# Turning the input of a two-layer decoder trunk once, and giving VectorE the low parts of the weights in three stages

## The chip, the cores and the metric

The kernel runs on one core of a Trainium2 chip, as one launch. The metric is the device time of one execution in microseconds (us), taken over several runs; a profile is one more execution of the same program, with its own time.

## The reference, cut to what matters

Two layers on x of 1024 tokens by 1024 features, all in fp32. Layer 0 is an mLSTM mixer and a squared-ReLU MLP, layer 1 is latent attention on shared keys and values and the same kind of MLP. The change touches layer 0's mixer and its first residual:

```python
cond = silu(c)
sh1, sc1, g1, sh2, sc2, g2 = split(cond @ ada_w[0] + ada_b[0], 6)      # adaLN vectors
h = rmsnorm(x, norm_g[0, 0]) * (1 + sc1) + sh1                         # first normalisation
q, k, v, ig, fg, og = split(h @ w_in)                                  # 8 heads
hh = mlstm_chunkwise(q, k, v, ig + b0, fg + b1)                        # chunks of 128 tokens
y = (rmsnorm(hh, head_g) * sigmoid(og)) @ w_out
x = x + g1 * rmsnorm(y, norm_g[0, 1])                                  # first residual
h2 = rmsnorm(x, norm_g[0, 2]) * (1 + sc2) + sh2
x = x + g2 * rmsnorm(sqrelu_mlp(h2), norm_g[0, 3])
# layer 1: the same frame around latent attention, then its MLP
```

## The kernel before

Tokens go in two halves of 512. Activations lie with features on the partitions: a tensor of one half is 8 blocks (`KD`) of 128 features by 512 tokens. The input arrives with tokens on the partitions and so has to be turned, 128 by 128, by TensorE.

**Split precision.** Each fp32 operand of a product is kept as a high part (a ScalarE cast to the reduced fp32 kind of TensorE, `hi`) and a low part (x - hi, `lo`). A product (`mm3`, L236 to L238) is three matmuls: low weight by high activation, high by low, high by high. An activation's low part is made by VectorE or GpSimd. A weight comes in blocks of 512 KB on SyncE's DMA queue (`wload`, issue at L216) into one of four buffers `raw`; `wsplit` then lets ScalarE cast the high part (`wh`, L193) and VectorE or GpSimd, taking turns, make the low part (`wl`, L195). A list of one entry, `low[0]`, names one engine for all low parts while it is set. There is room for four split weights.

**Layer 0 up to the first residual**, in the order of the program:

1. `vector_columns` and the load of half 0's x (`x0`, L299). `first_norm`: ScalarE squares the rows (L496), VectorE scales each row by its rstd (L503), TensorE turns the scaled rows (32 transposes, L524), ScalarE copies them into `xT0` (L1655).
2. `ada_first(j)` makes the first adaLN vectors for features 512j to 512j + 511, from weight columns loaded beside (TensorE products L326 and L338, VectorE sums L363/L365). `modulate0(…, j)` then makes u = xT * A + sh on VectorE (L1662), the high part on ScalarE (L1663), the low part (L1665). Half 0's q/k products (`qk_pairs`) run in two halves of the features around this.
3. `gates_in` (the gates' product), woven with steps of `bgs`, the background stream that makes the other adaLN vectors out of 512 KB blocks (loads L358 into the same `raw` buffers, VectorE multiply-adds L365 into `tma`, transposes L345, sum L347).
4. `load_x1` (half 1's x), then `v_in` (products for v) woven with `intra0` (chunk-local part of the mLSTM: gate chains on 8 partitions around L701 to L786, small products L749 to L772) and `bgs`.
5. `scale_x1` (squares L510, scaling L520 on VectorE and GpSimd), then `in_turn` lays side by side the output gates `og0` of half 0, the chunk recurrence `chunks0` and, as a fill advanced at two of three steps, `norm0`: half 1's transposes (L530) into PSUM, one ScalarE activation that scales and shifts (L532), and the two parts (L534 to L538).
6. Half 1: `gates_in`, then q/k and v products woven with `intra0`, `split_o` (o split in parts, L784 to L786) of half 0 and `bgs`.
7. `wout` of half 0 beside `chunks0` of half 1; then `og0` of half 1 with `split_o` of half 1 and `p0`; then `wout` of half 1 woven with `p0`. `p0 = post(...)` is half 0's residual (`residual`, add at L941) and second normalisation (`normed`, L478 to L485). Half 1's, `p1`, runs inside the MLP of half 0.

The residual takes its x from a source: `x_rows` loads the rows once more (L895) and turns each block with four transposes (L901) into PSUM; layer 1 and the MLPs use `x_ahead`, which loads 512 KB blocks of the running x^T from a DRAM scratch `xs`.

**What sets the order.** A scheduler lays the instructions of each engine in one fixed order by its own estimate of times; priorities (`prompt`), `issue_after` and `paced` push it. Each engine and SyncE's DMA queue work through their lists in that order; a DMA that waits for a buffer holds all that stand behind it. PSUM has tags `ps`, `pc` and `pm` with two buffers each (`pm` has two banks). SBUF tags are `tmp` (3), `tmc` (6), `k4` (24), `hd` (8).

Of the kernel before, what the change touches and what calls it, by code (L numbers as in the profile page):

```python
# [17 lines left out]
P = 128  # L18
# [29 lines left out]
def drain(*gens):  # L48
    for g in gens:
        for _ in g:  # L50
            pass
# [31 lines left out]
def kernel(  # L83
# [42 lines left out]
    def hd(dt=F32):  # L126
        return sb.tile([P, 1024], dt, tag="hd", bufs=HD, name=f"hd_{next(uid)}")
# [10 lines left out]
    def tmc(dt=F32):  # L138
        return sb.tile([P, 512], dt, tag="tmc", bufs=TMC, name=f"tmc_{next(uid)}")
# [4 lines left out]
    def small(n, dt=F32):  # L144
        return sb.tile([P, n], dt, tag=f"sm{n}", bufs=6, name=f"sm_{next(uid)}")
# [4 lines left out]
    def pc():  # L150
        return pp.tile([P, 512], F32, tag="pc", bufs=2, name=f"pc_{next(uid)}")

    def pm():
        return pp.tile([P, 2, 512], F32, tag="pm", bufs=2, name=f"pm_{next(uid)}")

    def const(shape, dt, name):
        return sb.tile(shape, dt, tag=name, bufs=1, name=name)
# [271 lines left out]
    def rsqrt_(y, v, t):  # L429

        nc.scalar.activation(t, v, AF.Ln)
        nc.scalar.activation(y, t, AF.Exp, scale=-0.5)
        nc.vector.tensor_mul(t, y, y)
        nc.vector.scalar_tensor_tensor(t, t, -0.5, v, ALU.mult, ALU.mult)
        nc.vector.scalar_tensor_tensor(y, t, 1.5, y, ALU.add, ALU.mult)
# [53 lines left out]
            if k % 4 == 3:  # L489
                yield 1  # L490

    def scale_rows(xt):
        st = small(4)
        for t in range(4):
            junk = pm()
            nc.scalar.activation(  # L496
                junk.rearrange("p a b -> p (a b)"), xt[t], AF.Square, accum_out=st[:, t : t + 1]
            )
        v, y, w = small(4), small(4), small(4)
        nc.vector.tensor_scalar(v, st, 1.0 / D, EPS, ALU.mult, ALU.add)  # L500
        rsqrt_(y, v, w)
        for t in range(4):
            nc.vector.tensor_scalar(xt[t], xt[t], y[:, t : t + 1], None, ALU.mult)  # L503

    def scale_x1(x1):
# [7 lines left out]
        v, y, w = small(4), small(4), small(4)  # L513
        nc.vector.tensor_add(v, st[:, 0:4], st[:, 4:8])
        nc.vector.tensor_scalar(v, v, 1.0 / D, EPS, ALU.mult, ALU.add)
        rsqrt_(y, v, w)
        for g in range(2):
            for t in range(4):
                e = nc.gpsimd if t % 2 else nc.vector
                e.tensor_scalar(x1[g][t], x1[g][t], y[:, t : t + 1], None, ALU.mult)  # L520

    def turn(xt, pt, k):
        for t in range(4):
            nc.tensor.transpose(pt[:, ts(t, P)], xt[t][:, ts(k, P)], ident)  # L524

    def norm0(h, xt, A, sh):
        for k in range(KD):
            pt = ps()
            for t in range(4):
                nc.tensor.transpose(pt[:, ts(t, P)], xt[k // 4][t][:, ts(k % 4, P)], ident)  # L530
            u = tmc()
            nc.scalar.activation(u, pt, AF.Identity, bias=sh[:, k : k + 1], scale=A[:, k : k + 1])  # L532
            if k % 2:
                nc.vector.tensor_copy(h.hi[k], u)  # L534
            else:
                nc.scalar.copy(h.hi[k], u)
            e = nc.vector if k % 2 else nc.gpsimd
            e.tensor_sub(h.lo[k], u, h.hi[k].bitcast(F32))  # L538
            yield


# [121 lines left out]
    def og0(hf, alloc):  # L663
        hf.gs = FH(F32, alloc)
        for k in range(NH):
            pt = proj_fm(w_in, 2064 + k * P, hf.h)
            g = hf.gs[k]
            nc.scalar.activation(g, pt, AF.Exp, scale=-1.0)
            nc.scalar.activation(g, g, AF.Ln, bias=1.0)
            nc.scalar.activation(g, g, AF.Exp, scale=-1.0)  # L670
            nc.vector.tensor_scalar(g, g, col(HG + k, 1), None, ALU.mult)
            yield
# [206 lines left out]
    def wout(w, o, store, wide=False):  # L879

        for m in range(KD):
            pt = proj_fm(w, m * P, o, (lambda: pm()[:, 0]) if wide and m % 2 else ps)
            store(m, pt)
            yield


    xs = scratch([D, S], "xs")
    xs_blk = lambda k, half: xs[ts(k, P), ts(half, H)]

    def x_rows(half):  # L890

        xt = []
        for t in range(4):
            a = hd() if half else k4()[:, :1024]
            nc.sync.dma_start(a, x_of[half * 4 + t])  # L895
            xt.append(a)

        def blk(k):
            pt = pc()
            for t in range(4):  # L900
                nc.tensor.transpose(pt[:, ts(t, P)], xt[t][:, ts(k, P)], ident)  # L901
            return pt

        return blk

    def x_cols(half):
        def blk(k):
# [3 lines left out]

        return blk

    def x_ahead(alloc):


        def src(half):
            t = [alloc() for _ in range(4)]
            for b in range(4):
                nc.sync.dma_start(  # L920
                    t[b], xs[2 * b * P : (2 * b + 2) * P, ts(half, H)].rearrange("(k p) n -> p k n", p=P)
                )
            return lambda k: t[k // 2][:, k % 2]

        return src
# [721 lines left out]

    def first_norm():

        scale_rows(x0)  # L1650
        xT = FH(claim=True)
        for k in range(KD):
            pt = pc()
            turn(x0, pt, k)
            nc.scalar.copy(xT[k], pt)  # L1655
        return xT

    def modulate0(h, xT, j):
        A, sh = A0, adac(0, SH1)
        for k in range(4 * j, 4 * j + 4):  # L1660
            u = tmc()
            nc.vector.tensor_scalar(u, xT[k], A[:, k : k + 1], sh[:, k : k + 1], ALU.mult, ALU.add)  # L1662
            nc.scalar.copy(h.hi[k], u)  # L1663
            e = nc.gpsimd if j and k % 2 else nc.vector
            e.tensor_sub(h.lo[k], u, h.hi[k].bitcast(F32))  # L1665
            yield

    def w_raw(b):
# [7 lines left out]
        return [t.rearrange("p (a b) -> p a b", b=256) for t in wsplit(r, D)]  # L1676

    vector_columns()
    xT0 = first_norm()
    drain(ada_first(0, k4))  # L1680

    w0 = [w_raw(b) for b in range(3)]
# [26 lines left out]
    def in_turn(wide, steps, fill):  # L1709

        traced = nc.cur_bb.bb.instructions
        last = [None]

        def go(gen):
            top = traced[-1]
            if last[0] is None:
                r = next(gen, StopIteration)
            else:
                with tc.issue_after(last[0]):
                    r = next(gen, StopIteration)  # L1720
            for i in reversed(traced):
                if i is top:
                    break
                if i.engine == pe_last[0].ins.engine:
                    last[0] = i
                    break
            return r

        n = 0
        while go(steps) is not StopIteration:  # L1730

            if n % 3 < 2:
                go(wide)
                next(fill, None)
            n += 1
        drain(wide)

    bgs = chain(bg0, bg1)
    drain(qk_pairs(hfs[0], w0, modulate0(hfs[0].h, xT0, 1)))
    drain(with_bg(gates_in(hfs[0]), bgs, 1))  # L1740
    x1 = load_x1()
    drain(weave(with_bg(v_in(hfs[0]), bgs, 1), intra0(hfs[0]), 1.5))
    scale_x1(x1)
    hfs[1].h = Split()
    n1 = norm0(hfs[1].h, x1, A0, adac(0, SH1))
# [235 lines left out]
```

## Time and profile before

| | us |
|---|---|
| three runs | 2413.01, 2415.41, 2417.33 |
| their median | 2415.41 |
| the profiled execution | 2414.08 |
| its span in the trace | 2412.3 |

In the profile PE is TensorE's matmuls, PEld its weight loads, DVE is VectorE, ACT ScalarE, POOL GpSimd, SP SyncE, and SPq a DMA queue's own waits. L12 is line 12 of the kernel. A group row reads: line, engine, operation, out<-in, partitions by elements, count, then busy time, mean ns, and the idle time of the engine ahead of these with what ended it. A timeline row has the start, the busy time, and the instruction; brackets give the idle time ahead of it. PEclk is the granted TensorE clock as a share of full speed.

### The profile page before, as it was taken

The page shows a single profiled execution, that of the slowest core. Times are in us where ns is not written, and L with a number is a line of the kernel's source. Part 1 is how long each engine was busy: PE and PEld are TensorE (multiplying, and loading weights), DVE is VectorE, ACT ScalarE, POOL GpSimd, SP SyncE. Part 2 cuts the span into 40 slices and gives each one's busy share as a digit, 9 for nine tenths or more (in the row PEclk, how much of TensorE's full clock was granted, in tenths as well). Part 3 has the DMA queues.
Part 4 walks back from the last instruction along what each step waited for, and adds up shares of the span by engine and source line. Part 5 has one row for each costly group of instructions (what it writes and reads, how often), then busy time and mean ns, then how long its engine had stood idle before and what let it go on. Part 6 is the DMA issues. An engine that isn't in the chain of part 4 may idle for free.

```text
span 2412.3 us, 30656 instructions
## 1 busy us (share of the span) xinstructions
PE 2369.8 (98%) x11669; PEld 1950.5 (81%) x11669; DVE 1476.4 (61%) x2269; ACT 1049.5 (44%) x1706; POOL 435.5 (18%) x269
## 2 busy tenths in 40 slices
PE   7999999999999999999999999999999999999998
PEld 5887787788888887888888877888888888888886
DVE  6576766958665667866664967554555385253335
ACT  4355334645333354434444554434444443443333
POOL 2131221300000000233421100332221102121121
PEclk9999999999999999999999999999999999999999
DMA  7442564444654745555543454774424454354431
GB/s 267 147 130 63 176 191 131 150 133 141 197 175 130 246 133 182 155 168 176 185 131 110 145 161 153 243 250 139 157 97 135 119 162 122 109 188 134 143 103 62
DMA packets 373843, 370.30 MB, mean 154 GB/s; under 512 B 24163, under 2 KB 282272, under 8 KB 373696
## 3 DMA queue, kind: packets, MB, share of 16 engines
q1 hardware_dynamic: 373408, 368.24, 48.6%
q8 instruction: 92, 1.51, 0.3%
q14 instruction: 55, 0.45, 0.1%
q0 software_dynamic: 288, 0.10, 0.0%
HBM read 313.24 MB, written 55.05 MB: 153 GB/s over the span
## 4 chain that ended last, share of the span: by engine, by line
PE 88%; DVE 6%; DMA 3%; ACT 2%; issue 1%; POOL 0%; SPq 0%; DVEq 0%; ACTq 0%
PE ps L236 16%; PE ps L237 16%; PE ps L238 16%; PE pm L236 9%; PE pm L238 9%; PE pm L237 9%; DMA raw<-in_mlp_w_dram 2%; PE pc L1456 1%; PE pc L236 1%; PE pm L811 1%; PE pc L238 1%; PE pc L237 1%; PE pm L1342 1%; PE pm L1336 1%; PE pm L1338 1%
## 5 line engine op out<-in xcount | busy, mean ns | idle before, releaser
L193 ACT CAST wh<-raw 128x1024 fp32r<-128x1024 f32 (+2 forms) x366 | 375.8, 1032 | 740.2 <-PE ps L236 356.3
L195 POOL TENSOR_TENSOR wl<-raw,wh 128x1024 fp32r<-128x1024 f32 (+2 forms) x158 | 379.8, 2409 | 1522.3 <-ACT wh L193 1356.7
L236 PE MATMUL ps<-k,wl 128*128 128x512 f32 x1528 | 611.4, 400 | 6.5 <-DVE wl L195 3.3
L237 PE MATMUL ps<-k,wh 128*128 128x512 f32 x1528 | 601.5, 394 | 0.0
L238 PE MATMUL ps<-k,wh 128*128 128x512 f32 x1528 | 600.8, 393 | 0.0
L195 DVE TENSOR_TENSOR wl<-raw,wh 128x1024 fp32r<-128x1024 f32 (+1 forms) x208 | 270.0, 1301 | 285.1 <-ACT wh L193 278.1
L236 PEld LDWEIGHTS ps<-k,wl 128*128 128x128 f32 x1528 | 287.0, 188 | 74.3 <-DVE wl L195 5.0
L238 PEld LDWEIGHTS ps<-k,wh 128*128 128x128 f32 x1528 | 287.0, 188 | 67.5 <-issue 0.5
L237 PEld LDWEIGHTS ps<-k,wh 128*128 128x128 f32 x1528 | 287.4, 188 | 63.0 <-issue 1.9
L203 DVE TENSOR_TENSOR k<-k,pm 128x512 f32<-128x512 f32 (+1 forms) x254 | 210.7, 859 | 130.3 <-PE pm L238 129.5
L476 DVE TENSOR_TENSOR hd<-tmp,hd 128x512 fp32r<-128x512 f32 x128 | 120.9, 945 | 205.5 <-ACT hd L475 205.2
L236 PE MATMUL pm<-hd,wl 128*128 128x512 f32 x512 | 201.8, 394 | 0.5 <-ACT hd L475 0.5
L237 PE MATMUL pm<-hd,wh 128*128 128x512 f32 x512 | 199.7, 390 | 0.7 <-DVE hd L476 0.7
L238 PE MATMUL pm<-hd,wh 128*128 128x512 f32 x512 | 200.0, 391 | 0.0
L236 PE MATMUL pm<-wh,hd 128*128 128x512 f32 x488 | 192.4, 394 | 2.8 <-ACT raw L1348 2.5
L237 PE MATMUL pm<-wl,hd 128*128 128x512 f32 x488 | 191.3, 392 | 0.0
L238 PE MATMUL pm<-wh,hd 128*128 128x512 f32 x488 | 191.1, 392 | 0.0
L365 DVE SCALAR_TENSOR_TENSOR tma<-raw,cond,tma 128x512 f32<-128x512 f32 x168 | 130.4, 776 | 20.9 <-DMA raw<-in_ada_w_dram 12.1
L1348 ACT ACTIVATE raw<-pm,sm 128x128 f32<-128x128 f32 (+3 forms) x64 | 47.4, 741 | 157.0 <-DVE sm L1347 126.7
L237 PEld LDWEIGHTS pm<-hd,wh 128*128 128x128 f32 x512 | 96.2, 188 | 21.6 <-DVE hd L476 1.0
L236 PEld LDWEIGHTS pm<-hd,wl 128*128 128x128 f32 x512 | 96.1, 188 | 21.4 <-ACT hd L475 0.9
L238 PEld LDWEIGHTS pm<-hd,wh 128*128 128x128 f32 x512 | 96.1, 188 | 21.0
(359 smaller groups left out, 3603.2 us busy)
## 6 DMA issues: line engine op xcount, KB each, us to landing
raw<-in_mlp_w_dram SPq DMA_DIRECT2D x256, 512.0 KB, 4.3
raw<-in_ada_w_dram SPq DMA_DIRECT2D x80, 512.0 KB, 4.4
raw<-in_a_w_in_dram SPq DMA_DIRECT2D x48, 512.0 KB, 4.6
xs<-k SPq DMA_DIRECT2D x40, 256.0 KB, 4.6
raw<-in_kv_ada_w_dram SPq DMA_DIRECT2D x16, 512.0 KB, 4.0
raw<-in_a_w_out_dram SPq DMA_DIRECT2D x16, 512.0 KB, 4.7
kd<-k SPq DMA_DIRECT2D x32, 256.0 KB, 3.5
vd<-k SPq DMA_DIRECT2D x32, 256.0 KB, 5.0
```

What stands on the lines that cost most here:

```text
L193: nc.scalar.copy(hi[:, :n], r[:, :n])
L195: i = e.tensor_sub(lo[:, :n], r[:, :n], hi[:, :n].bitcast(F32))
L203: return f(*a, **k)
L236: nc.tensor.matmul(o, ll, rh, start=start, stop=False)
L237: nc.tensor.matmul(o, lh, rl, start=False, stop=False)
L238: pe_last[0] = nc.tensor.matmul(o, lh, rh, start=False, stop=stop)
L365: nc.vector.scalar_tensor_tensor(acc, r[:, kk], cond[:, k : k + 1], acc, ALU.mult, ALU.add)
L476: nc.vector.tensor_sub(lo, u, hi.bitcast(F32))
L811: nc.tensor.matmul(nv[:, r, i], hf.PT[p_][:, r, cs], v[:, 2 * p_ + r], start=g == 0, stop=True,)
L1336: nc.tensor.matmul(o[:, :w], ql, kh, start=True, stop=False)
L1338: nc.tensor.matmul(o[:, :w], qT, kk[1][:, ks], start=False, stop=False)
L1348: nc.scalar.activation(pr[:, :n], f, AF.Exp, bias=m, scale=SCALE, accum_out=l)
```

## The change

- The rows of x are no longer scaled. `rms_x0` and `rms_x1` give only rstd per token; `along_tokens` spreads it over the partitions (four matmuls with the identity and a ScalarE copy), and the modulation multiplies by it: u = xT * A * rstd on VectorE in one instruction, then `split_mod` makes the high part with the shift on ScalarE and the low part on VectorE, for every block.
- x^T is kept in two DRAM scratches `xt_d`: half 0's four blocks of 512 KB behind the first q/k products in the program, half 1's eight blocks of 256 KB out of `norm0`, which now copies each turned block out of PSUM first.
- The first residual of both halves reads x^T from there by `x_ahead(…, True)`; `x_rows` is gone.
- `low[0]` is VectorE in `v_in`/`intra0` of half 0 and from `gates_in` to `v_in`/`intra0` of half 1.
- `gates_in` of half 0 is no longer woven with `bgs`.
- `in_turn` advances its fill at each step.
- Half 1's output gates alternate between `ps` and one bank of `pm` (`one_pm`).

```diff
+    def one_pm():
+        return pm()[:, 0]
...
-    def scale_rows(xt):
+    def along_tokens(dst, y):
+        pt = pc()
+        for t in range(4):
+            nc.tensor.matmul(
+                pt[:, ts(t, P)], y[:, t : t + 1].to_broadcast([P, P]), ident, start=True, stop=True
+            )
+        nc.scalar.copy(dst, pt)
+        return dst
+    def rms_rows(v):
+        nc.vector.tensor_scalar(v, v, 1.0 / D, EPS, ALU.mult, ALU.add)
+        y, w = small(4), small(4)
+        rsqrt_(y, v, w)
+        return y
...
-        v, y, w = small(4), small(4), small(4)
-        nc.vector.tensor_scalar(v, st, 1.0 / D, EPS, ALU.mult, ALU.add)
-        rsqrt_(y, v, w)
-        for t in range(4):
-            nc.vector.tensor_scalar(xt[t], xt[t], y[:, t : t + 1], None, ALU.mult)
+        return rms_rows(st)
...
-        for g in range(2):
-            for t in range(4):
-                e = nc.gpsimd if t % 2 else nc.vector
-                e.tensor_scalar(x1[g][t], x1[g][t], y[:, t : t + 1], None, ALU.mult)
...
-    def norm0(h, xt, A, sh):
+    xt_d = [scratch([D, H], f"xt{i}") for i in range(2)]
+    def norm0(h, xt, y, A, sh):
+        rstd = along_tokens(tmp(), y)
         for k in range(KD):
             pt = ps()
-            for t in range(4):
-                nc.tensor.transpose(pt[:, ts(t, P)], xt[k // 4][t][:, ts(k % 4, P)], ident)
-            u = tmc()
-            nc.scalar.activation(u, pt, AF.Identity, bias=sh[:, k : k + 1], scale=A[:, k : k + 1])
-            if k % 2:
-                nc.vector.tensor_copy(h.hi[k], u)
-            else:
-                nc.scalar.copy(h.hi[k], u)
-            e = nc.vector if k % 2 else nc.gpsimd
-            e.tensor_sub(h.lo[k], u, h.hi[k].bitcast(F32))
+            turn(xt[k // 4], pt, k % 4)
+            a, u = tmp(), tmc()
+            nc.scalar.copy(a, pt)
+            nc.sync.dma_start(xt_d[1][ts(k, P)], a)
+            nc.vector.scalar_tensor_tensor(u, pt, A[:, k : k + 1], rstd, ALU.mult, ALU.mult)
+            split_mod(h.hi[k], h.lo[k], u, sh[:, k : k + 1])
             yield
...
-            pt = proj_fm(w_in, 2064 + k * P, hf.h)
+            pt = proj_fm(w_in, 2064 + k * P, hf.h, one_pm if hf.i and k % 2 else ps)
...
-    def x_rows(half):
...
-    def x_ahead(alloc):
+    def x_ahead(alloc, first=False):
         def src(half):
             t = [alloc() for _ in range(4)]
+            of = xt_d[half] if first else xs[:, ts(half, H)]
             for b in range(4):
                 nc.sync.dma_start(
-                    t[b], xs[2 * b * P : (2 * b + 2) * P, ts(half, H)].rearrange("(k p) n -> p k n", p=P)
+                    t[b], of[2 * b * P : (2 * b + 2) * P].rearrange("(k p) n -> p k n", p=P)
                 )
...
-        scale_rows(x0)
+        y = rms_x0(x0)
...
-        return xT
+        return xT, along_tokens(Cst.rearrange("p a b -> p (a b)")[:, :H], y)
...
             u = tmc()
-            nc.vector.tensor_scalar(u, xT[k], A[:, k : k + 1], sh[:, k : k + 1], ALU.mult, ALU.add)
-            nc.scalar.copy(h.hi[k], u)
-            e = nc.gpsimd if j and k % 2 else nc.vector
-            e.tensor_sub(h.lo[k], u, h.hi[k].bitcast(F32))
+            nc.vector.scalar_tensor_tensor(u, xT[k], A[:, k : k + 1], rs0, ALU.mult, ALU.mult)
+            split_mod(h.hi[k], h.lo[k], u, sh[:, k : k + 1])
...
             if n % 3 < 2:
                 go(wide)
-                next(fill, None)
+            next(fill, None)
...
     drain(qk_pairs(hfs[0], w0, modulate0(hfs[0].h, xT0, 1)))
-    drain(with_bg(gates_in(hfs[0]), bgs, 1))
+    for b in range(4):
+        nc.sync.dma_start(
+            xt_d[0][2 * b * P : (2 * b + 2) * P].rearrange("(k p) n -> p k n", p=P), xT0.t[b]
+        )
+    drain(gates_in(hfs[0]))
     x1 = load_x1()
+    low[0] = nc.vector
     drain(weave(with_bg(v_in(hfs[0]), bgs, 1), intra0(hfs[0]), 1.5))
-    scale_x1(x1)
+    low[0] = None
+    y1 = rms_x1(x1)
...
+    low[0] = nc.vector
     drain(gates_in(hfs[1]))
...
     drain(weave_n(with_bg(main, bgs, 1.7), intra0(hfs[1]), 0.8))
+    low[0] = None
...
-    p0 = post(hfs[0], y0, B0, x_rows, A1, adac(0, SH2))
+    p0 = post(hfs[0], y0, B0, x_ahead(k4v, True), A1, adac(0, SH2))
...
-    p1 = post(hfs[1], y1, B0, x_rows, A1, adac(0, SH2))
+    p1 = post(hfs[1], y1, B0, x_ahead(hdv, True), A1, adac(0, SH2))
```

More of the change, by code (lines that the diff above doesn't have):

```diff
@@ L490, in normed, with rms_x0 @@
                 yield 1
-    def scale_rows(xt):
+    def along_tokens(dst, y):
[11 more added lines that the diff above has]
+        return y
+    def rms_x0(xt):
         st = small(4)
@@ L498, in scale_rows, with rms_x1 @@
             )
-        v, y, w = small(4), small(4), small(4)
-        nc.vector.tensor_scalar(v, st, 1.0 / D, EPS, ALU.mult, ALU.add)
-        rsqrt_(y, v, w)
-        for t in range(4):
-            nc.vector.tensor_scalar(xt[t], xt[t], y[:, t : t + 1], None, ALU.mult)
-    def scale_x1(x1):
+        return rms_rows(st)
+    def rms_x1(x1):
         st = small(8)
@@ L512, in scale_x1 @@
                 )
-        v, y, w = small(4), small(4), small(4)
+        v = small(4)
         nc.vector.tensor_add(v, st[:, 0:4], st[:, 4:8])
-        nc.vector.tensor_scalar(v, v, 1.0 / D, EPS, ALU.mult, ALU.add)
-        rsqrt_(y, v, w)
-        for g in range(2):
-            for t in range(4):
-                e = nc.gpsimd if t % 2 else nc.vector
-                e.tensor_scalar(x1[g][t], x1[g][t], y[:, t : t + 1], None, ALU.mult)
+        return rms_rows(v)
     def turn(xt, pt, k):
@@ L881, in wout @@
         for m in range(KD):
-            pt = proj_fm(w, m * P, o, (lambda: pm()[:, 0]) if wide and m % 2 else ps)
+            pt = proj_fm(w, m * P, o, one_pm if wide and m % 2 else ps)
             store(m, pt)
@@ L888 @@
     xs_blk = lambda k, half: xs[ts(k, P), ts(half, H)]
-    def x_rows(half):
[L892 to L904, printed above, removed]
     def x_cols(half):
@@ L1678 @@
     vector_columns()
-    xT0 = first_norm()
+    xT0, rs0 = first_norm()
     drain(ada_first(0, k4))
@@ L1739 @@
     drain(qk_pairs(hfs[0], w0, modulate0(hfs[0].h, xT0, 1)))
-    drain(with_bg(gates_in(hfs[0]), bgs, 1))
+    for b in range(4):
[3 more added lines that the diff above has]
+    drain(gates_in(hfs[0]))
     x1 = load_x1()
+    low[0] = nc.vector
     drain(weave(with_bg(v_in(hfs[0]), bgs, 1), intra0(hfs[0]), 1.5))
-    scale_x1(x1)
+    low[0] = None
+    y1 = rms_x1(x1)
     hfs[1].h = Split()
-    n1 = norm0(hfs[1].h, x1, A0, adac(0, SH1))
+    n1 = norm0(hfs[1].h, x1, y1, A0, adac(0, SH1))
     in_turn(og0(hfs[0], hdv), chunks0(hfs[0]), n1)
     drain(n1)
+    low[0] = nc.vector
     drain(gates_in(hfs[1]))
```

## The prediction

> **What bounds the kernel now.** I read the page's busy shares and its chain first, then busy time by window, then TensorE's waits, then the timelines of the places where TensorE waits.
>
> ```profile
> span 2412.3 us, 30656 instructions
> PE 2369.8 (98%) x11669; PEld 1950.5 (81%) x11669; DVE 1476.4 (61%) x2269; ACT 1049.5 (44%) x1706; POOL 435.5 (18%) x269
> PE 88%; DVE 6%; DMA 3%; ACT 2%; issue 1%; POOL 0%; SPq 0%; DVEq 0%; ACTq 0%
> ```
>
> TensorE is busy 98% of the span and is 88% of the chain. So a gain is either TensorE work taken out, or one of TensorE's few waits. The windows (us, then busy us of PE, PEld, DVE, ACT, POOL, granted clock, DMA share, GB/s) and the waits (total, times, longest) show where these are.
>
> ```profile
> 0.00:25.00 25.00, 11.86 (x58) 7.45 (x58) 14.23 (x39) 13.24 (x23) 6.36 (x21) 1.00 0.95 337
> 117.70:121.10 3.40, 1.52 (x9) 0.99 (x9) 3.40 (x6) 2.81 (x8) 2.67 (x1) 1.00 0.61 186
> 121.10:124.50 3.40, 3.40 (x18) 3.40 (x17) 1.55 (x2) 0.31 (x1) 0.00 (x0) 0.50 0.88 273
> 124.50:127.90 3.40, 3.40 (x31) 2.92 (x30) 1.75 (x4) 2.82 (x6) 2.38 (x1) 1.00 0.56 194
> 150.00:225.00 75.00, 75.00 (x452) 61.10 (x452) 49.70 (x126) 39.87 (x86) 22.73 (x13) 1.00 0.23 64
> 250.00:275.00 25.00, 22.60 (x126) 16.88 (x126) 18.63 (x36) 8.07 (x17) 2.58 (x5) 1.00 0.55 160
> 300.00:375.00 75.00, 75.00 (x543) 66.13 (x542) 49.39 (x101) 25.09 (x53) 14.91 (x6) 1.00 0.60 178
> 425.00:450.00 25.00, 25.00 (x127) 20.65 (x126) 23.73 (x31) 16.58 (x25) 7.00 (x3) 1.00 0.60 184
> 450.00:475.00 25.00, 25.00 (x110) 20.07 (x109) 24.47 (x33) 17.22 (x26) 9.22 (x11) 1.00 0.36 111
> 500.00:525.00 25.00, 25.00 (x112) 20.04 (x111) 16.62 (x23) 12.78 (x20) 0.00 (x0) 1.00 0.24 71
> ```
>
> ```profile
> PE pc L524 <- DVE k L503: 5.2, 1, 5.2
> PE ps L236 <- DVE wl L195: 3.3, 3, 1.6
> PE ps L236 <- ACT k L203: 1.6, 1, 1.6
> PE ps L237 <- POOL wl L195: 1.3, 1, 1.3
> PE pc L749 <- ACT tmc L756: 0.5, 1, 0.5
> PE pc L338 <- DVE tmc L365: 0.4, 1, 0.4
> PE pc L338 <- DVE ada L341: 0.3, 1, 0.3
> ```
>
> Wherever the change reaches, TensorE waits only at the start, around 70, around 118 and between 250 and 275. From 150 to 225 and from 300 to 375 it never stops.
>
> **Transposes of the residual's x: -7.0.** The 64 transposes of L901 go; x^T comes by DMA instead, in as many loads of 512 KB as the x rows took.
>
> ```profile
> L901 PE MATMUL pc<-ident,k x32: 270/272/273, 427.0 to 447.1; 128*128 128x128 f32 x32
> L901 PE MATMUL pc<-ident,hd x32: 270/272/273, 517.0 to 542.3; 128*128 128x128 f32 x32
> ```
>
> ```profile
> 440.32 0.39 PE L236 MATMUL ps<-k,wl 128*128 128x512 f32 x1
> 441.01 0.60 PE L901 MATMUL pc<-ident,k 128*128 128x128 f32 x4
> 441.36 0.48 PE L236 MATMUL ps<-k,wl 128*128 128x512 f32 x1
> 442.14 0.39 PE L236 MATMUL ps<-k,wl 128*128 128x512 f32 x1
> ```
>
> A duration of 0.272 overlaps its neighbours, so I price by starts. Four transposes move the next matmul by 441.36 - 441.01 = 0.35, and the triple behind them takes 0.78 instead of 0.69: 0.44 for a block. Two halves of 8 blocks: 16 x 0.44 = 7.0. The second half (517 to 542) leaves in full, since VectorE is at 16.62 of 25 there. In the first, VectorE is busy 23.73 + 24.47 = 48.20 of 50: TensorE may shed 1.8 of its 3.5 before VectorE is the bound, so up to 1.7 comes back; there the output product of half 1 also waits for VectorE's and GpSimd's split of its operand. I take +0.5 (0 to +1.7): TensorE shows no wait there, which speaks for the low end.
>
> **The start: -0.7 (+1 to -5.2).** x is no longer scaled before it is turned, so the 5.2 wait for L503 goes. But the DMA engines hold the pace (tenths of busy share, slices of 1.5 us, then GB/s):
>
> ```profile
> DMA  0599999999999999999999999999390000065038
> GB/s 0 98 391 354 398 371 375 385 391 391 386 386 384 351 348 356 379 389 388 385 385 392 393 312 348 354 345 167 37 302 23 0 0 0 0 156 194 0 60 281
> ```
>
> ```profile
> 27.89 0.50 PE L236 MATMUL pm<-k,wl 128*128 128x512 f32 x1 [1.49 <-ACT k L1663]
> 39.05 1.02 PE L338 MATMUL pc<-ones,tmc 128*128 128x1 f32 x8 [0.37 <-DVE tmc L365]
> 26.64 1.92 DVE L1662 TENSOR_SCALAR tmc<-k,mods,ada 128x512 f32<-128x512 f32 x4
> L485 DVE SCALAR_TENSOR_TENSOR hd<-hd,mods,tmc 128x512 f32<-128x512 f32 x8 | 5.4, 748 | 0.0
> ```
>
> Loads run without a gap to 42, and the first modulation, for which the first q/k matmul waits at 27.89, needs the adaLN vectors that they bring. The transposes only move into time in which TensorE waits for data anyway. What is left are two waits behind VectorE (0.4 + 0.3), which has the scaling less to do: -0.7. Against it, the modulation's first step becomes a scalar_tensor_tensor: 0.748 instead of 1.92 / 4 = 0.48, four times +0.27, hence the +1. Spreading rstd along the tokens is eight matmuls more (0.44 for four): the first four lie in that wait, the other four stand in half 1's normalisation: **+0.4**.
>
> The store of x^T (2 MB, at 386 GB/s 5.4 us) stands on SP's queue ahead of the weights of the second half of the q/k products. The DMA engines fall quiet at 45 and stay so to 52, so the stores fit, and those weights land as late as 49. An estimate from this row gives about 1 us of slack: 0, at worst +3.
>
> **The stalls around 70 and 118: -1.65, -1.9, -1.4.** In both a weight of v_in comes late.
>
> ```profile
> 67.64 1.05 ACT L193 CAST wh<-raw 128x1024 fp32r<-128x1024 f32 x1 [8.42 <-DMA raw<-in_a_w_in_dram]
> SPq L216 <- DVE tma L365: 31.4, 4, 26.3
> 117.45 2.91 POOL L195 TENSOR_TENSOR wl<-raw,wh 128x1024 fp32r<-128x1024 f32 x1 [34.83 <-ACT wh L193]
> ```
>
> At 67.64 ScalarE's queue stood 8.42 at a cast whose weight was loaded behind adaLN blocks; the evictions behind it held TensorE's PSUM for 1.6 (waits, L203). Now gates_in of half 0 draws no adaLN steps, and in the changed kernel's instruction order the weight loads stand ahead of them: the 1.65 goes. At 117, SP's queue (waits from 50 to 125) had waited 26.3 for the raw buffer that VectorE's L365 frees, then GpSimd took 2.91 for the low part. In the new order the pair behind that wait is loaded and split ahead of the chain of the gates, with the low part on VectorE: 0.5 + 1.3 of waits, or 3.40 - 1.52 = 1.9, goes.
>
> Right behind this stall the granted clock was 0.50 for 3.4 us: 18 matmuls instead of 31. At full speed they take 18 x 3.40 / 31 = 1.97, so 1.43 was lost. I take it that the slow stretch follows the stall (-1.4); if not, 0. [...]
>
> **VectorE makes the low parts in both v_in/intra stages: +0.5 (-3.3 to +3).**
>
> ```profile
> L195 POOL TENSOR_TENSOR wl<-raw,wh 128x1024 fp32r<-128x1024 f32 (+2 forms) x158 | 379.8, 2409 | 1522.3 <-ACT wh L193 1356.7
> L195 DVE TENSOR_TENSOR wl<-raw,wh 128x1024 fp32r<-128x1024 f32 (+1 forms) x208 | 270.0, 1301 | 285.1 <-ACT wh L193 278.1
> L195 DVE TENSOR_TENSOR wl<-raw,wh 128x1024 fp32r<-128x1024 f32 x10 | 15.6, 1561 | 16.4 <-ACT wh L193 16.4
> L195 POOL TENSOR_TENSOR wl<-raw,wh 128x1024 fp32r<-128x1024 f32 x9 | 22.3, 2478 | 96.5 <-ACT wh L193 96.5
> ```
>
> The last two rows are 250 to 375 alone. Nine low parts move to VectorE, 9 x 1.30 = 11.7; its ten there fall from 1.56 to 1.30, since GpSimd's no longer run beside them, and give back 2.6. VectorE has room: 18.63 of 25 and 49.39 of 75. A weight's low part comes in 1.3 instead of 2.4, but behind whatever VectorE has queued, the gates' chain included. Best, the three waits on VectorE's low parts go (-3.3); worst, two of 1.5 stand in a row (+3); +0.5 since TensorE has no wait from 300 on.
>
> [...]
>
> **Half 1's normalisation: +0.3 (0 to +3).** A PSUM bank is now released by a ScalarE copy and a VectorE multiply (0.75) instead of one activation; VectorE has 49.70 of 75 and TensorE no wait there, so I take half a block. x^T's eight stores stand on SP between w_in loads; at 0.23 DMA share nothing waits. Output gates alternating between PSUM kinds: 0, hidden by the same full TensorE.
>
> **Sum:** -7.0 + 0.5 - 0.7 + 0.4 - 1.65 - 1.9 - 1.4 + 0.5 + 0.3 = -10.95. The profiled execution took 2414.08; that gives 2403.1. The three runs shown have their median 1.3 above it (2415.41): **2404.5**. A measurement of this kernel can tell about 0.2%, 4.8 us.
>
> **Rivals.**
> *Slower: VectorE becomes the bound in half 1's q/k and v_in.* The 10 + 9 weights of 250 to 375 each come one low part late, SP's weight loads queueing behind raw buffers that VectorE frees: 19 x 1.30 = 24.7, 2429. It decides once VectorE reaches 25 of 25 in these windows; for it, three waits on its L195 already; against, 68 of 100 busy plus 9.1. Chance 0.11.
> *Little change: the stalls form again elsewhere* (the adaLN blocks still hold the raw buffers, and must come sometime) and VectorE takes 1.7 in 425 to 475: 1.65 + 1.9 + 1.4 + 1.2 = +6.2, 2410.7. For it, the 26.3 wait is no shorter by itself; against, the weights' new places ahead. Chance 0.21.
> *The x^T store delays the q/k weights,* +3, and a half-clock stretch of 1.4 behind it: 2408.9. Chance 0.08.
> *The start's wait goes in full,* 4.5 more: 2400. Against it, the DMA row. Chance 0.10.
> *The transposes cost nothing now* (they fill gaps): 2411.5; excluded by 25.00 of 25 busy and the shift of 0.44.
>
> **How the numbers follow.** Forecast 0.50 (2401 to 2408 with its bounds), the rest as above. Faster by over 0.2% (under 2410.6): forecast, start, store and nearly half of the second rival, 0.77; slower (over 2420.2): 0.09; same 0.14. The range takes in all but the slower rival and the tail of little change: low 2397 (the start's case with 3 of low-part waits gone), high 2414.
>
> **What would show it.** Right: no L901 in the trace and PE's count lower by about 56; no PE wait at 68 to 70 nor 117 to 121; clock 1.00 from 100 to 125; PE still full from 425 to 475; the first q/k matmul near 27.5. Wrong: VectorE at 24 or more of 25 in 250 to 375 with TensorE waiting for wl; a TensorE wait near 50 behind a DMA; waits for split_o's blocks near 455.

## The result, and the profile after

| | before | after |
|---|---|---|
| median, us (22 runs each) | 2415.59 | 2418.04 |
| lowest to highest | 2413.01 to 2418.51 | 2416.45 to 2422.01 |
| span of the profile | 2412.3 | 2415.3 |

The ratio is 1.0012 (95% interval 1.0006 to 1.0017): slower by 0.12%, a small loss that is clear of the spread of these runs. A gain of 11 us was forecast, to 2404.5, and the range ended at 2414.

The page of the changed kernel, its span, busy shares and chain:

```profile
span 2415.3 us, 30563 instructions
PE 2368.1 (98%) x11621; PEld 1946.3 (81%) x11621; DVE 1488.3 (62%) x2283; ACT 1050.3 (43%) x1712; POOL 396.7 (16%) x247
PE 83%; DVE 7%; DMA 6%; ACT 3%; issue 1%; POOL 0%; SPq 0%; DVEq 0%; ACTq 0%
```

TensorE's share of the chain fell from 88 to 83%. Less work is in the kernel, and more waiting. Two windows of before, and then windows of after (us, then busy us of PE, PEld, DVE, ACT, POOL, granted clock, DMA share, GB/s):

```profile
50.00:125.00 75.00, 71.48 (x441) 61.41 (x440) 40.53 (x70) 23.75 (x47) 10.61 (x9) 0.98 0.46 149
225.00:300.00 75.00, 71.24 (x414) 58.68 (x413) 59.07 (x95) 26.42 (x51) 16.75 (x10) 1.00 0.50 152
```

```profile
50.00:125.00 75.00, 75.00 (x496) 66.08 (x495) 46.78 (x75) 26.08 (x55) 3.50 (x6) 1.00 0.46 149
225.00:300.00 75.00, 73.98 (x462) 61.41 (x461) 61.50 (x99) 27.17 (x55) 8.31 (x6) 1.00 0.50 155
425.00:450.00 25.00, 22.57 (x97) 17.67 (x95) 24.48 (x28) 12.89 (x19) 13.85 (x3) 1.00 0.73 223
450.00:475.00 25.00, 19.71 (x74) 14.79 (x74) 22.52 (x29) 17.43 (x28) 8.16 (x10) 0.93 0.20 64
475.00:500.00 25.00, 22.33 (x88) 18.13 (x89) 12.41 (x10) 8.43 (x12) 5.40 (x2) 0.86 0.49 128
700.00:725.00 25.00, 23.04 (x96) 18.43 (x96) 18.61 (x24) 9.69 (x12) 0.00 (x0) 0.93 0.60 180
```

The stalls around 70 and 118 are gone, as forecast: TensorE is full from 50 to 125. Those between 225 and 300 have become smaller. But from 425 to 500, where it never stopped before but for 0.7, it idles, and for part of that time it runs at half clock (0.50 from 454.67 to 458.08 and from 475.16 to 481.99). A fresh stall stands at 717. TensorE's waits of the changed kernel from 420 to 500 (total, times, longest):

```profile
PE ps L239 <- POOL wl L198: 5.4, 1, 5.4
PE ps L239 <- ACT k L796: 2.2, 1, 2.2
PE pc L469 <- DVE tmc L465: 1.8, 1, 1.8
PE ps L240 <- POOL k L797: 1.0, 1, 1.0
```

To add up by stage I use TensorE's time over its floor: the time from each matmul's start to the next's, less the usual distance for its width in these traces (0.228 us for 512 columns, 0.172 for 384, 0.117 for 256, 0.108 for 130, 0.109 for 128, else 0.05), summed over one profile. It holds waits and half clock alike, and leaves the matmuls themselves out. The last two columns are two experiments told below.

| us of the span | before | after | bg_three | bg3_low |
|---|---|---|---|---|
| 0 to 50 | 19.6 | 18.3 | 19.4 | 18.3 |
| 50 to 125 | 7.4 | 1.0 | 1.0 | 1.0 |
| 125 to 225 | 1.3 | 2.1 | 2.1 | 2.0 |
| 225 to 300 | 5.3 | 2.5 | 2.9 | 2.6 |
| 300 to 425 | 3.1 | 3.6 | 3.9 | 4.3 |
| 425 to 500 | 2.4 | 16.3 | 9.8 | 2.4 |
| 500 to 650 | 2.6 | 2.5 | 2.4 | 2.1 |
| 650 to 750 | 1.2 | 6.0 | 0.9 | 1.0 |
| the rest | 38.2 | 37.3 | 38.1 | 38.1 |
| all | 81.2 | 89.7 | 80.6 | 71.8 |

Before 425 the changed kernel has won 9.3 on these terms. It loses 13.9 from 425 to 500 and 4.8 around 717. The list of matmuls is 48 rows shorter, 5.2 us at 0.109 each (64 transposes less; the eight matmuls of `along_tokens` show as 16 rows), and that does not make it up.

**What stands on VectorE there.** VectorE's adaLN multiply-adds (L365 before, L368 after), in windows of before and then of after (us, DVE busy, clock, DMA share, GB/s):

```profile
340.00:400.00 60.00, 5.25 (x7) 1.00 0.33 97
400.00:440.00 40.00, 0.00 (x0) 1.00 0.53 173
```

```profile
340.00:400.00 60.00, 0.00 (x0) 1.00 0.22 63
400.00:440.00 40.00, 5.16 (x7) 1.00 0.66 213
```

Seven operations have moved some 50 us later, into the stage of half 0's first residual. The timeline there, TensorE's row first and then VectorE's:

```profile
412.47 0.60 PE L348 MATMUL pc<-ident,tma 128*128 128x128 f32 x4
...
414.14 2.55 DVE L366 TENSOR_SCALAR tma<-raw,cond 128x512 f32<-128x512 f32 x1
416.62 0.68 DVE L471 TENSOR_SCALAR tmc<-pc 128x512 f32<-128x512 f32 x1
...
419.01 0.68 DVE L436 TENSOR_TENSOR tmc<-tmc 128x512 f32<-128x512 f32 x1
419.62 0.74 DVE L368 SCALAR_TENSOR_TENSOR tma<-raw,cond,tma 128x512 f32<-128x512 f32 x1
420.28 0.68 DVE L437 SCALAR_TENSOR_TENSOR tmc<-tmc,tmc 128x512 f32<-128x512 f32 x1
...
432.46 4.89 DVE L937 TENSOR_TENSOR hd<-hd,k 128x512 f32<-128x512 f32 x8
...
440.21 8.68 DVE L465 TENSOR_TENSOR tmc<-tmc,tmc 128x512 f32<-128x512 f32 x6
...
451.34 1.22 DVE L795 TENSOR_TENSOR hd<-hd,k 128x1024 f32<-128x1024 f32 x1
```

Between the steps of the residual's rstd (L471, L436, L437, L438) stands one adaLN operation each. The additions of x (L937), no longer paced by transposes, run as a block of eight, and six of the next sums (L465) take 8.68. The third block of the mLSTM output (L795) is multiplied at 451.34. ScalarE's list has a cast of that block (L796) ahead of two evictions of output gates, and it waits 6.24; TensorE waits behind it:

```profile
452.59 1.04 ACT L796 CAST k<-hd 128x1024 fp32r<-128x1024 f32 x1 [6.24 <-DVE hd L795]
```

Why the seven operations moved can be read in the code. A chunk of an adaLN vector is seven steps of `bgs`: four loads with their multiply-adds into `tma`, two empty steps, and then its turn by transposes (L345 before, L348 after). `tma` has one buffer. Counting the steps: before, the stream has drawn 56 and then 7 steps where `p0` is made, a whole number of chunks. In the changed kernel the gates of half 0 draw three fewer, so it is 56 and then 4. The chunk's sums are complete in `tma`, but its turn comes only beside half 1's output gates (412.47 above), and the next chunk's sums cannot begin before that. No run gives `tma` a second buffer; that the one buffer holds the chunk back is read from the code and this timeline.

### The profile page after: what moved, and what is told of

It reads as the page before. It is cut to its first block, busy times and chain, and to the rows that moved or that the text cites. A ratio compares the mean times of both kernels' runs of the same rounds, so it can differ in the third digit from the quotient of the medians.

```text
span 2415.3 us, 30563 instructions
## 1 busy us (share of the span) xinstructions
PE 2368.1 (98%) x11621; PEld 1946.3 (81%) x11621; DVE 1488.3 (62%) x2283; ACT 1050.3 (43%) x1712; POOL 396.7 (16%) x247
## 4 chain that ended last, share of the span: by engine, by line
PE 83%; DVE 7%; DMA 6%; ACT 3%; issue 1%; POOL 0%; SPq 0%; DVEq 0%; ACTq 0%
PE ps L239 15%; PE ps L240 15%; PE ps L241 15%; PE pm L239 9%; PE pm L240 9%; PE pm L241 9%; DMA raw<-in_mlp_w_dram 4%; PE pc L1452 1%; ACT wh L196 1%; DVE wl L198 1%; PE pc L239 1%; PE pc L240 1%; PE pc L241 1%; PE pm L822 1%; PE pm L1338 1%
## 5 line engine op out<-in xcount | busy, mean ns | idle before, releaser
L239 PE MATMUL ps<-k,wl 128*128 128x512 f32 x1496 | 601.0, 402 | 7.6 <-POOL wl L198 5.4
L198 POOL TENSOR_TENSOR wl<-raw,wh 128x1024 fp32r<-128x1024 f32 (+2 forms) x146 | 356.1, 2443 | 1505.6 <-ACT wh L196 1197.2
L241 PE MATMUL ps<-k,wh 128*128 128x512 f32 x1496 | 590.8, 395 | 0.0
L240 PE MATMUL ps<-k,wh 128*128 128x512 f32 x1496 | 589.1, 394 | 1.0 <-POOL k L797 1.0
L198 DVE TENSOR_TENSOR wl<-raw,wh 128x1024 fp32r<-128x1024 f32 (+1 forms) x220 | 280.2, 1276 | 292.7 <-ACT wh L196 288.1
L241 PEld LDWEIGHTS ps<-k,wh 128*128 128x128 f32 x1496 | 281.9, 188 | 66.7 <-issue 0.2
L240 PEld LDWEIGHTS ps<-k,wh 128*128 128x128 f32 x1496 | 282.7, 189 | 63.9 <-POOL k L797 1.5
L368 DVE SCALAR_TENSOR_TENSOR tma<-raw,cond,tma 128x512 f32<-128x512 f32 x168 | 127.2, 757 | 9.8 <-DMA raw<-in_ada_w_dram 8.0
```

What stands on the lines that cost most here:

```text
L198: i = e.tensor_sub(lo[:, :n], r[:, :n], hi[:, :n].bitcast(F32))
L239: nc.tensor.matmul(o, ll, rh, start=start, stop=False)
L240: nc.tensor.matmul(o, lh, rl, start=False, stop=False)
L241: pe_last[0] = nc.tensor.matmul(o, lh, rh, start=False, stop=stop)
L368: nc.vector.scalar_tensor_tensor(acc, r[:, kk], cond[:, k : k + 1], acc, ALU.mult, ALU.add)
```

## The experiments

All times are medians of five or more executions, with the ratio to the kernel before. That kernel was measured anew beside each four of them, in the order of the table, with 2415.3, 2414.3 and 2415.1. Times from different fours can thus be apart by about 1 us for that alone. The floors are read in one profiled execution each, which lies up to 3.3 from its kernel's median (bg3_low_h0: 2408.30 against 2405.00).

| kernel | us | ratio, 95% interval |
|---|---|---|
| bg_three | 2406.89 | 0.9962 (0.9949 to 0.9976) |
| rows_back | 2411.38 | 0.9981 (0.9972 to 0.9989) |
| og_ps | 2417.14 | 1.0007 (0.9998 to 1.0016) |
| no_bg_og | 2429.07 | 1.0055 (1.0042 to 1.0067) |
| bg3_low | 2399.88 | 0.9941 (0.9927 to 0.9954) |
| bg3_rows0 | 2401.81 | 0.9949 (0.9936 to 0.9961) |
| bg3_turns | 2416.18 | 1.0007 (0.9998 to 1.0016) |
| bg_back | 2409.57 | 0.9979 (0.9971 to 0.9988) |
| bg3_low_rows | 2406.48 | 0.9967 (0.9955 to 0.9980) |
| bg3_low_h0 | 2405.00 | 0.9963 (0.9950 to 0.9975) |
| og_low_dve | 2412.51 | 0.9990 (0.9981 to 0.9999) |
| bg3_low_ps | 2403.72 | 0.9957 (0.9945 to 0.9970) |

**bg_three.** To the changed kernel:

```diff
     low[0] = None
+    for _ in range(3):
+        next(bgs)
     drain(bg0)
```

> The changed kernel, with three more steps of the background stream of adaLN vectors drawn at the end of half 1's q/k and v stage, so that the first residual's stage meets the stream where it met it before. Background theory (the three steps that the gates of half 0 no longer draw leave the last sum of a chunk into the output gates, and the next chunk's eleven VectorE operations then stand between the steps of half 0's residual): those operations move ahead of 400 us, the residual's first multiplies start near 417 instead of 422.8, TensorE's waits from 440 to 480 fall from 14 us over its floor to about 4, time 2408 (2406 to 2411). Pacing theory (without the transposes the additions of x run in one block ahead of the split of half 1's mLSTM output): the waits stay, 2417. PSUM theory (alternating output gates reorder the evictions): they stay, 2417.

11.2 less than the changed kernel. Its adaLN multiply-adds, and its windows:

```profile
340.00:400.00 60.00, 5.26 (x7) 1.00 0.34 98
400.00:440.00 40.00, 0.00 (x0) 1.00 0.62 203
...
425.00:450.00 25.00, 25.00 (x110) 19.98 (x109) 24.96 (x30) 14.39 (x22) 9.17 (x3) 1.00 0.66 210
450.00:475.00 25.00, 18.53 (x77) 14.69 (x77) 23.44 (x28) 18.06 (x28) 11.62 (x11) 0.91 0.21 65
...
700.00:725.00 25.00, 25.00 (x112) 20.40 (x112) 12.22 (x15) 9.07 (x12) 0.00 (x0) 1.00 0.52 147
```

The multiply-adds are back at 340 to 400, TensorE is full from 425 to 450, and the stall at 717 is gone too. The background theory holds, but it had the size wrong on one point: from 450 to 475 a wait is left (9.4 over the floor from 440 to 480, not about 4; the changed kernel has 15.1). The multiplies of the residual began 2.3 earlier (420.55), not 6.

**rows_back.** `x_rows` comes back as it was before.

```diff
-    p0 = post(hfs[0], y0, B0, x_ahead(k4v, True), A1, adac(0, SH2))
+    p0 = post(hfs[0], y0, B0, x_rows, A1, adac(0, SH2))
...
-    p1 = post(hfs[1], y1, B0, x_ahead(hdv, True), A1, adac(0, SH2))
+    p1 = post(hfs[1], y1, B0, x_rows, A1, adac(0, SH2))
```

> The changed kernel, with the residual's x loaded as rows and turned by TensorE again in both halves; x^T is still stored. Pacing theory: the split's blocks come in time again, the waits from 440 to 480 go, 64 transposes come back at 7.0: 2418 - 11 + 7 = 2414, with under 4 us over the floor from 425 to 500. Background theory and PSUM theory: the waits stay, and the transposes fill part of them; 2418 to 2422, with over 8 us over the floor.

Faster than the changed kernel by 6.7, with more work. Over the floor from 425 to 500 stand 1.4, so the waits there go in this way too, although the stream's steps stay where they were; at 717 they stay (6.1 from 650 to 750). The adaLN operations alone, then, do not make the waits of 440 to 475: they do so together with an order in which the residual's work stands in blocks. The pacing theory was right on the mechanism and 2.6 too high in its time.

**og_ps.**

```diff
-            pt = proj_fm(w_in, 2064 + k * P, hf.h, one_pm if hf.i and k % 2 else ps)
+            pt = proj_fm(w_in, 2064 + k * P, hf.h, ps)
```

> The changed kernel, with all output gates of half 1 in the one PSUM kind again. PSUM theory: the waits from 440 to 480 go, 2408. Background and pacing theory: no change or slower, 2417 to 2421, since one more output must wait for an eviction.

Nearly the changed kernel's time (2418.04). The waits are not removed but collected in one, of 9.7 behind a low part on VectorE:

```profile
425.00:450.00 25.00, 15.27 (x58) 11.92 (x57) 24.48 (x31) 11.92 (x19) 9.28 (x2) 0.80 0.67 211
```

The PSUM theory fell.

**no_bg_og.** Eight `next(bgs)` beside half 1's output gates are left out; the MLP draws them.

> The changed kernel without the eight background steps beside half 1's output gates; they are made later, in the MLP of half 0. Background theory: the stage from 400 to 480 gains as much as with the three steps, 2408, unless the chunk costs the same in the MLP. Theory that VectorE bounds this stage by the residual and the split alone: the waits fall by no more than 3, 2415 to 2417.

The waits from 425 to 450 go as in bg_three (0.8 over the floor), but two waits, of 5.3 and 5.1, come at 864 and 870, in the shared keys and values that need these vectors. The stream can't be put off: 2429.

**bg_three's remaining wait.** TensorE waits once, 6.5 from 467 on, for a low part by GpSimd. ScalarE's list at that place, GpSimd's and VectorE's, in bg_three:

```profile
459.69 5.36 ACT L481 ACTIVATE k<-hd,ada 128x512 fp32r<-128x512 f32 x8 [3.87 <-DVE hd L488]
464.96 1.03 ACT L196 CAST wh<-raw 128x1024 fp32r<-128x1024 f32 x1
465.90 0.58 ACT L210 COPY k<-ps 128x512 f32<-128x512 f32 x1
...
466.07 7.47 POOL L198 TENSOR_TENSOR wl<-raw,wh 128x1024 fp32r<-128x1024 f32 x1 [7.48 <-ACT wh L196]
...
464.22 5.38 DVE L482 SCALAR_TENSOR_TENSOR k<-hd,ada,k 128x512 fp32r<-128x512 f32 x8
469.52 1.22 DVE L198 TENSOR_TENSOR wl<-raw,wh 128x1024 fp32r<-128x1024 f32 x1
470.65 3.44 DVE L465 TENSOR_TENSOR tmc<-tmc,tmc 128x512 f32<-128x512 f32 x2
```

GpSimd was idle 7.48 before its row, for the cast. All eight modulations of half 0 stand ahead of the next weight's cast and of the evictions that free TensorE's PSUM. The low part that TensorE waits for then takes 7.47 beside VectorE's unbroken run, where GpSimd takes 2.40 undisturbed (the changed kernel, 1001.42): 5.1 more, of a wait of 6.5. The next one takes 2.8, so that the 5.1 of the expectation below is the mean of two unequal ones. By size either of the two could make most of the wait: the modulations ahead of the cast take 5.36, the low part 5.1 more than undisturbed. Two kernels put casts between the modulations.

**bg3_low**, bg_three with

```diff
     p0 = post(hfs[0], y0, B0, x_ahead(k4v, True), A1, adac(0, SH2))
+    low[0] = nc.vector
...
     follow[0], pace[0] = False, None
+    low[0] = None
```

> The changed kernel with three more background steps ahead of the first residual, and VectorE making all low parts of the weights from half 1's output gates to the end of its output product. Order theory (the wait of 6.5 at 466 comes from ScalarE's list, in which all eight modulations of half 0 stand ahead of the casts and evictions of the output product, and from GpSimd's low parts of 5.1 behind them): in this kernel's list the casts and evictions stand between the modulations, so TensorE's time over its floor from 450 to 475 falls from 7.7 to under 2.5, and the time to 2402 (2400 to 2404). Theory that VectorE bounds this stage by its sum of work: it gets about three low parts more, 3.7 us, the wait stays or grows, 2407 to 2411.

2399.9, the fastest kernel of this study, with 1.5 over the floor from 450 to 475. Its windows and the same stretch of ScalarE's list:

```profile
450.00:475.00 25.00, 24.54 (x105) 19.33 (x104) 19.28 (x27) 17.34 (x26) 2.66 (x9) 1.00 0.30 87
475.00:500.00 25.00, 25.00 (x110) 20.34 (x109) 9.79 (x11) 9.75 (x14) 0.00 (x0) 1.00 0.45 129
...
459.27 1.38 ACT L481 ACTIVATE k<-hd,ada 128x512 fp32r<-128x512 f32 x2 [3.00 <-DVE hd L488]
460.72 1.05 ACT L196 CAST wh<-raw 128x1024 fp32r<-128x1024 f32 x1
461.68 0.58 ACT L210 COPY k<-ps 128x512 f32<-128x512 f32 x1
462.15 1.34 ACT L481 ACTIVATE k<-hd,ada 128x512 fp32r<-128x512 f32 x2
```

VectorE makes more low parts and is yet busy for less (19.28 of 25 where it had 23.44). The sum of its work did not bound the stage. This run does not separate the order of ScalarE's list from the low parts' move off GpSimd: it changes both.

**bg3_rows0**, bg_three with `x_rows` for half 0 alone.

> The changed kernel with the three background steps, and with half 0's residual taking x from rows turned by TensorE; half 1's still from the stored x^T. Order theory: here too the casts stand between the modulations, the wait at 466 goes (-6), 32 transposes come back (+3.5), 2404.5 (2403 to 2406). VectorE-bound theory: the wait shrinks only by the 3.5 that TensorE arrives later, 2407.

2401.8; 0.7 over the floor from 450 to 475. Here GpSimd still makes low parts, and the wait is gone with the casts standing between the modulations. But the low part at that place takes 2.75 (461.23) and not 7.47, so this run changes both too. It came out 2.7 faster than I expected; half 0's 32 transposes seem to cost less than the 3.5 that they are priced at, and no run separates that.

**bg3_turns**, bg_three without the two `low[0] = nc.vector` of the change.

> The changed kernel with the three background steps, and with VectorE and GpSimd taking turns at the low parts in all stages, as before the change. If VectorE's low parts took the waits at 118 and from 250 to 275 away: those come back, +2 to +5, 2409 to 2412. If the weights' earlier places in SyncE's list did it: no change, 2406 to 2408.

9.3 slower than bg_three, twice what I expected; the floors of the two profiles differ by 5.3 only. Over the floor 2.9 from 50 to 125, 6.2 from 225 to 300 and 5.8 from 300 to 425, where bg_three has 1.0, 2.9 and 3.9. From 225 to 425 VectorE's low parts are worth more than was gained there (12.0 without them, 6.8 in bg_three, 8.4 in the kernel before). From 50 to 125 they are worth less: 4.5 of the 6.4 stay gained without them, and the stall at 118 does not come back (0.2 over the floor from 110 to 125; 3.9 in the kernel before).

**bg_back**, the changed kernel with

```diff
-    drain(gates_in(hfs[0]))
+    drain(with_bg(gates_in(hfs[0]), bgs, 1))
```

> The changed kernel with half 0's gates woven with the background stream again; the first residual meets the stream at the same step as with three more steps drawn later. If the stream in the gates made the waits near 68 and 118: +1.65 and up to +3.3 for the other and its half-clock stretch against the kernel with three steps drawn later, 2408.5 to 2412. If not: 2406 to 2408.

2.7 slower than bg_three: the stream left out of the gates is worth that, where it is made up for elsewhere. Left out without making up, as in the change, it costs 8.5 (2418.04 against 2409.57). The waits near 68 and 118 come back only in small part: 0.9 over the floor from 62 to 75 and 0.9 from 110 to 125, where the kernel before has 2.0 and 3.9 and bg_three 0.4 and 0.0. So neither the stream nor the engine of the low parts made these stalls alone, and no run withdraws both.

**bg3_low_rows, bg3_low_h0, og_low_dve, bg3_low_ps.** Four edits to take the terms apart: bg3_low with `x_rows` in both halves; bg3_low with VectorE and GpSimd in turns in half 1's stage; the changed kernel with bg3_low's two lines but without the three steps; bg3_low with all output gates in `ps`.

> The changed kernel with three more background steps and VectorE's low parts up to the output product of half 1, but with x for the residual of both halves loaded as rows and turned by TensorE again. The ScalarE list keeps casts between the modulations. If each block of four transposes costs TensorE its 0.44: 16 blocks, +7.0 on 2399.9, 2407 (2405.5 to 2408), with no new wait from 400 to 550. If the transposes fill gaps: 2400 to 2402.

6.6 slower than bg3_low (5.8 if each is taken against the kernel before beside it). The price of the 64 transposes, 7.0, was right within what these medians tell.

> The same kernel with x^T from DRAM, but VectorE and GpSimd take turns at the low parts from half 1's gates to its v products; VectorE makes them all in half 0's stage and beside half 1's output gates. If half 1's stage carries the gain of VectorE's low parts: TensorE's time over its floor from 225 to 425 rises by 4 to 6, 2405 to 2408. If half 0's stage does: 2400 to 2402.

5.1 slower than bg3_low; over the floor it has 8.0 from 225 to 300 and 5.6 from 300 to 425, against 2.6 and 4.3. The rows of bg3_low_h0, where the stage's TensorE is busy for 71.45 and 123.50 against 73.92 and 124.47 in bg3_low:

```profile
225.00:300.00 75.00, 71.45 (x410) 57.57 (x409) 54.11 (x84) 27.11 (x52) 16.15 (x10) 0.98 0.44 135
300.00:425.00 125.00, 123.50 (x772) 104.63 (x771) 85.59 (x175) 50.89 (x100) 14.29 (x6) 1.00 0.55 166
```

> The changed kernel with VectorE's low parts from half 1's output gates to its output product, without the three background steps. Background and order theory: the wait of 5.4 at 472 goes, those from 444 to 453 and the ones at 717 stay, 2412 (2410 to 2414). Theory that VectorE's sum of work bounds the stage: 2418 to 2422.

2412.5: the wait behind GpSimd at 472 goes; 2.9 behind the cast of the third block (L796) stay at 449, 1.6 behind a modulation (L481) at 471, and 4.8 over the floor around 717. The two causes are separate and nearly add up: three steps -11.2, VectorE's low parts -5.5, both together -18.2.

> The kernel with three more background steps and VectorE's low parts up to half 1's output product, with half 1's output gates all in one PSUM kind. Its ScalarE list has five of the eight modulations ahead of the first cast of the output product. Order theory: a wait of 2 to 5 at that place, 2402 to 2405. If the alternating PSUM kinds had been worth something by themselves, waits behind evictions of the output gates between 400 and 440 come on top.

3.8 slower than bg3_low, as expected, but in another place: 2.8 behind an eviction of an output gate (L679) near 432 and nothing at the modulations. In the trace not five but all eight stand in a row ahead of the cast:

```profile
459.06 5.01 ACT L481 ACTIVATE k<-hd,ada 128x512 fp32r<-128x512 f32 x8
467.25 1.05 ACT L196 CAST wh<-raw 128x1024 fp32r<-128x1024 f32 x1 [3.17 <-PE ps L239]
```

Here the cast waits 3.17 for TensorE, behind the modulations, and VectorE makes the low part. So eight modulations ahead of a cast do not suffice for a wait, and the order theory failed here. What the wait of bg_three needs beside them, GpSimd's slow low part or TensorE's earlier arrival, stays open. The alternating PSUM kinds are worth something once the rest is in order.

## Why the prediction was wrong

**What failed first: the background stream in the gates.** The prediction took "gates_in of half 0 draws no adaLN steps" for a pure gain. It did not follow the three steps that the gates no longer draw. It named their return ("must come sometime") only in the rival of little change, at the price of the old stalls. In the runs they shift the stream against every later stage, and through the single `tma` one chunk of VectorE work falls between the steps of half 0's residual, and another wait falls at 717. Drawing the three steps later is worth 11.2, as much as the whole forecast gain.

**What failed second: the term of +0.5 (0 to +1.7) for the residual's stage.** It was read from VectorE's sum (48.20 busy of 50) and from TensorE's having no wait there. Both were poor guides. TensorE came 8 us earlier (half 1's first output gate is evicted at 402.07, before at 410.27) to a stage that had just kept up. With the stream where it was before (bg_three), TensorE still loses 9.8 from 425 to 500 where it lost 2.4: 7.4, not 0.5. Most of it is one wait for a low part that GpSimd makes in 7.47, behind a cast that stands behind eight modulations. With that mended (bg3_low) TensorE loses 2.4 again, VectorE is less busy, and the time is 7.0 lower. The share of the order and that of the slow low part are not separated. One sign of being wrong that the prediction named did show: TensorE waits for split_o's blocks, 1.0 at 445 (L797) and 2.2 at 451 (L796, by way of an eviction).

**A term with the wrong sign: VectorE's low parts.** Forecast +0.5 (-3.3 to +3) for both stages, worked out from half 1's rows. In the new kernel, taking turns instead costs 5.1 in half 1's stage (bg3_low_h0) and 9.3 in both (bg3_turns). Against the kernel before, TensorE's time over its floor from 225 to 425 fell by 2.3 (8.4 to 6.1). The prediction counted the waits that a profile names (3.3) and not the small ones.

**What was right.** The transposes: -7.0 forecast, -6.6 measured. The stalls near 70 and 118 went, and their half-clock stretch with them (clock 1.00 from 100 to 125): -4.95 forecast, 7.4 to 1.0 over the floor. The number was right; that the gates' stream and the low parts on VectorE did it is not shown, since neither stall comes back in full when one of the two is withdrawn (bg_back, bg3_turns). The start: -0.7 forecast, 19.6 to 18.3 over the floor; but the experiments, which leave the start as the changed kernel has it, lie between 18.3 and 19.7, so the size is within their spread. The first q/k matmul came at 27.60, where 27.5 was expected. The store of x^T brought no wait of TensorE near 50. The count of TensorE's rows fell by 48, not 56. The slower rival (VectorE as the bound of half 1's stage) did not happen: VectorE has 18.41 of 25 from 250 to 275 and 48.98 of 75 from 300 to 375.

Put together: the stages from 425 to 500 and around 717 lost 13.9 and 4.8 where 0.5 was forecast, 18.2 more. The two repairs together give the same (2418.04 to 2399.88). Gains before 425 that were larger than forecast hide part of it, and 13.5 is left between the forecast and the result. That the sums meet so well is partly luck, as each repair also changes other stages by about 1.

## What to carry to other kernels

A generator of background work that is drawn by count is a clock: take three draws out anywhere and all later draws move, so count the draws at the entrance of each later stage, and look for a single buffer that can turn a shift into a wait. A stage in which TensorE has no wait is not a stage with slack: a gain ahead of it is cashed only if the other engines' lists there can be passed through earlier too, and these must be read in their order (what stands ahead of the cast or the eviction) and row by row (a low part that takes three times its usual time), not by their sums.

## What the runs showed of the hardware that was not expected

In the changed kernel GpSimd's low part took 2.40 with no VectorE operation beside it (1001.42), and 5.3 to 8.1 at three places where VectorE's operations follow each other without a gap:

```profile
426.53 5.72 POOL L198 TENSOR_TENSOR wl<-raw,wh 128x1024 fp32r<-128x1024 f32 x1 [10.11 <-ACT wh L196]
437.83 5.32 POOL L198 TENSOR_TENSOR wl<-raw,wh 128x1024 fp32r<-128x1024 f32 x1 [5.58 <-ACT wh L196]
...
469.54 8.07 POOL L198 TENSOR_TENSOR wl<-raw,wh 128x1024 fp32r<-128x1024 f32 x1 [6.09 <-ACT wh L196]
```

VectorE's additions L465 took 8.68 for six at 440.21, with GpSimd working beside them up to 445.96, and 0.68 for the single one at 449.60, with GpSimd idle. In bg_three GpSimd's low part stands from 466.07 to 473.54, 7.47 long, while VectorE's operations follow each other without a gap until 471.3. It ends 2.2 after that, and VectorE's next operation, the second of the two at 470.65, takes 2.65 instead of 0.68. So both engines' operations took longer side by side, by 5.1 and 2.0 here. What makes them do so is not shown: no run sets a single pair of them against each other.

The granted clock was about half behind some stretches in which TensorE was partly busy, and full behind another. Windows of the changed kernel, each stall with what follows:

```profile
717.40:720.80 3.40, 1.44 (x9) 0.97 (x8) 3.39 (x4) 2.85 (x5) 0.00 (x0) 1.00 0.50 161
720.80:724.20 3.40, 3.40 (x10) 2.59 (x9) 3.08 (x5) 1.40 (x2) 0.00 (x0) 0.52 1.05 309
447.85:451.26 3.41, 1.58 (x6) 0.57 (x4) 3.31 (x6) 0.00 (x0) 0.00 (x0) 1.00 0.43 145
451.26:454.67 3.41, 1.25 (x5) 0.73 (x5) 2.30 (x3) 2.08 (x4) 0.00 (x0) 1.00 0.50 151
454.67:458.08 3.41, 3.41 (x10) 2.62 (x9) 2.11 (x5) 3.06 (x6) 0.00 (x0) 0.50 0.48 157
```

1.44 busy of 3.40 was followed by 3.4 us at 0.52, and 1.52 of 3.40 by 3.4 us at 0.50 in the kernel before (117.70 to 124.50); 1.58 of 3.41 was followed by a window at 1.00, and the 1.25 of that window by one at 0.50. In the 3.41 us at 0.50 from 454.67, 10 matmuls ran; in the next 3.41, at 1.00, 16 (458.08 to 461.49). So half clock stood behind three of these four stretches; if it is put down to them, they cost more than their own length. What the clock follows is not shown: no run changes how busy TensorE is in such a stretch and nothing else.
